# Sparse-attention indexer of a hybrid decoder step: the new tokens' index keys turned ahead of the last row block, their index products in one run, the head sums in four column groups

## The chip, the cores and the metric

The kernel runs on one core of a Trainium2 chip. The metric is the device time of one execution in microseconds (us), taken as the median of several executions. A core has five engines with a queue each: TensorE (matrix products; PE in the profile, its weight loads PEld), VectorE (DVE), ScalarE (ACT), GpSimd (POOL) and SyncE (SP, which only issues DMAs). An engine works through its queue in the order that the program was built with. Products are written to PSUM, a small memory that VectorE and ScalarE read.

## The reference, cut to what matters

One step of a decoder layer for 1024 prompt tokens and for 8 sequences with 4 new tokens each. The layer has sparse attention and retention side by side, merged by gates. The sparse attention first scores every key with a small "indexer" and then keeps the 256 best keys of each query:

```python
def index_scores(qi, wi, ki):
    s = jnp.einsum('bqhd,bsd->bqhs', qi, ki)               # 4 index heads of 64
    w = wi * (N_HEADS_IDX ** -0.5 * HEAD_DIM_IDX ** -0.5)
    return jnp.einsum('bqhs,bqh->bqs', jax.nn.relu(s), w)  # relu, then a weighted sum over the heads

def dsa_sample(...):                                        # the 8 sequences of new tokens
    ki_past = cache_kidx[page_table].reshape(DB, PAST_LEN, HEAD_DIM_IDX)
    ki_all = jnp.concatenate([ki_past, ki_new], axis=1)     # 1024 cached keys and 4 new ones
    idx, valid = select_keys(index_scores(qi, wi, ki_all), pos, topk)
    ...                                                     # attention over the chosen keys
```

All of it is in fp32. The index keys of the past lie in a paged cache, so that each sequence's 8 pages of 128 rows of 64 numbers must be gathered by a table.

## The kernel before, in words

**Order.** The program is traced in Python, and a planner lays out each engine's queue: from its own model of costs it takes, at each moment, the instruction that is ready and was traced first. `tc.issue_after(x)` keeps what it encloses behind instruction x on x's engine; it is an order in the queue and not a wait for x to end. The helper `together` (line 184) puts a list of products behind the first of them, so that once the first is placed the others are the next in line. Semaphores are set by the dependences of tiles: a tile of a pool with `bufs=n` takes the place of the n-th tile of its name before it, and waits until that one has been read.

**Projections.** Most of TensorE's time goes into projections of all 1056 tokens: 128 columns of weights at a time, the weights and the activations each split into a high and a low part (fp32r), three products per tile of 128 rows (lines 225 to 227), 24 products for each of three chunks of 352 tokens, 72 in all. ScalarE and VectorE or GpSimd split the weights one projection ahead (lines 210 and 211). The results lie in two PSUM banks `pj` in turn. The four "gate" projections (`gates`, lines 873 to 877, results copied by ScalarE in line 876) are traced behind the index stage, but are independent of it: the planner uses their products to fill TensorE while the index stage waits for other engines.

**Index stage, prompt.** The loop in lines 944 to 964 goes over row blocks b = 7 to 2 of 128 queries with widths of (b+1) x 128 keys, and over four heads: products into a two-bank PSUM tile `pl` (two such tiles, lines 952 and 953), relu by ScalarE into `rl` (two buffers, line 955), a weighted sum by VectorE into `SC[b]` (lines 957 and 959). Meanwhile GpSimd copies pages of the key cache (`copy_page`, line 582), one for each head after the first.

**Index stage, new tokens** (lines 967 to 1030). `gidx` holds the rows to be gathered. A small product with selectors builds `wsel`, which holds each query's head weights (lines 988 to 994). The 8 sequences are dealt with in two groups G of four:

- For each sequence b, GpSimd issues an indirect DMA of 256 KB into `kx` (line 1000, two buffers). TensorE turns it by four transposes into a PSUM bank `pt` (line 1006, two such banks), and ScalarE or VectorE copies the bank to `kp` (line 1008, five buffers).
- For each group, eight products of 64 rows, 32 query columns and 512 keys (line 1013) go to one `pl` tile: the halves o = 0 and 64 are the upper and lower 64 rows of the array and the two banks of the tile, b4 = 0 to 3 are four column groups of 32. Four more products handle the new keys in `kiT`, 32 columns wide (line 1016). Then ScalarE takes the relu into an `rl` tile (two strided pieces, line 1019, and a small one, line 1021).
- At the end, products with `wsel` sum over the heads of both groups: keys 0 to 511 in column group 0, keys 512 to 1023 in column group 1, the second group added to the first in PSUM (line 1026), and the 32 new keys (line 1027). ScalarE copies the two halves to `SCS` (line 1029), VectorE adds the mask to the new keys' part (line 1030).

Behind this stage its PSUM pool is closed and its banks are used by the retention stage (line 1142), and its SBUF is used by the search and by retention. The search for the 256th best score (`pick_all`, lines 1112 to 1136) reads `SC` and `SCS`; ScalarE and VectorE work through it in small steps during retention.

The lines that the change touches are 961 (where a mark is taken after each row block) and 995 to 1030.

Of the kernel before, what the change touches and what calls it, by code (L numbers as in the profile page):

```python
# [123 lines left out]
def _hybrid_step(ctx, tc, A, outs, dbg):  # L124
# [25 lines left out]
    def pl():  # L150
        return ps.tile([128, 1024], F32, name="pl", bufs=2)

    def pt():
        return ps.tile([128, 512], F32, name="pt", bufs=2)
# [89 lines left out]
    def last_on(engine):  # L244
        return next(i for i in reversed(nc.cur_bb.bb.instructions) if i.engine == engine)
# [638 lines left out]
    with ExitStack() as s1:  # L884
# [4 lines left out]
        with ExitStack() as s2:  # L889
# [52 lines left out]
            pages_of.append(pts)  # L942
            pages.extend((b, 2 * u + i) for G in (0, 1) for u in range(4) for b in range(4 * G, 4 * G + 4) for i in (0, 1))
            for b in range(7, 1, -1):
                W = (b + 1) * 128
                for h in range(4):
# [13 lines left out]
                    if h:  # L960
                        copy_page()
                if b == 7:
                    whole_row = scored.ins
# [31 lines left out]
            RL = []  # L995
            for G in (0, 1):
                KP = []
                for b in range(4 * G, 4 * G + 4):
                    kx = ip.tile([128, 8, 64], F32, name="kx", bufs=2)
                    nc.gpsimd.indirect_dma_start(  # L1000
                        out=kx.rearrange("p s d -> p (s d)"), out_offset=None,
                        in_=A["cache_kidx"][0].rearrange("g (r s) d -> (g r) (s d)", s=8),
                        in_offset=bass.IndirectOffsetOnAxis(ap=gidx[:, b:b + 1], axis=0))
                    p = pt()
                    for s in range(4):
                        nc.tensor.transpose(p[:, 128 * s:128 * s + 128], kx[:, 2 * s:2 * s + 2].rearrange("p a d -> p (a d)"), ident)
                    kp = ip.tile([128, 512], F32, name="kp", bufs=5)
                    (nc.vector.tensor_copy if b % 2 else nc.scalar.copy)(kp, p)
                    KP.append(kp)
                x, xn = pl(), pt()  # L1010
                for o in (0, 64):
                    for b4 in range(4):
                        nc.tensor.matmul(x[32 * b4:32 * b4 + 32, 8 * o:8 * o + 512], QF[o:o + 64, 4 * G + b4], KP[b4][o:o + 64],
                                         start=True, stop=True)
                for b4 in range(4):
                    nc.tensor.matmul(xn[32 * b4:32 * b4 + 32, :NS], QF[0:64, 4 * G + b4], kiT[0:64, T:], start=True, stop=True)
                rl = ip.tile([128, LK], F32, name="rl", bufs=2)
                for o in (0, 1):
                    nc.scalar.activation(rl[:, :PAST].rearrange("p (q s o) -> p o s q", s=4, o=2)[:, o],
                                         x[:, 512 * o:512 * o + 512].rearrange("p (s q) -> p s q", s=4), AF.Relu)  # L1020
                nc.scalar.activation(rl[:, PAST:], xn[:, :NS], AF.Relu)
                RL.append(rl)
            x, xn = pl(), pt()
            for G in (0, 1):
                for o, n0 in ((0, 0), (32, 512)):
                    nc.tensor.matmul(x[o:o + NS, n0:n0 + 512], wsel[:, G], RL[G][:, n0:n0 + 512], start=(G == 0), stop=(G == 1))
                nc.tensor.matmul(xn[:NS, :NS], wsel[:, G], RL[G][:, PAST:], start=(G == 0), stop=(G == 1))
            for o, n0 in ((0, 0), (32, 512)):
                nc.scalar.copy(SCS[:, n0:n0 + 512], x[o:o + NS, n0:n0 + 512])
# [714 lines left out]
```

## Time and profile before

| | |
|---|---|
| median of 3 runs | 1059.58 us (1057.87 to 1059.66) |
| profiled execution | 1059.82 us; 1058.2 us from its first to its last instruction |
| granted TensorE clock, mean | 0.995 |
| TensorE busy | 1034.1 us (98%) |
| weight loads of TensorE busy | 955.3 us (90%) |
| VectorE busy | 681.5 us (64%) |
| ScalarE busy | 451.7 us (43%) |
| GpSimd busy | 223.7 us (21%) |
| index stage, prompt row blocks | about 70 to 124 us from the start |
| index products of new tokens | 103.2 to 143.0 us |

A row of the order of time reads: start in us, length in us, engine, line of the kernel, operation, tile written <- tiles read, shapes, xcount of records that follow each other; in brackets the idle time before it and what ended that. A row of a group reads: line, engine, operation, tiles, shapes, xcount | time covered in us, mean length in ns | idle time before them. An fp32 product appears as two records; a transpose and an fp32r product as one. Records of TensorE overlap, since the next product starts before the last has drained; starts of neighbours say more than lengths. Only idle time of the engine that sets the end costs anything.

### The profile page before, as it was taken

The page shows a single profiled execution, that of the slowest core. Times are in us where ns is not written, and L with a number is a line of the kernel's source. Part 1 is how long each engine was busy: PE and PEld are TensorE (multiplying, and loading weights), DVE is VectorE, ACT ScalarE, POOL GpSimd, SP SyncE. Part 2 cuts the span into 40 slices and gives each one's busy share as a digit, 9 for nine tenths or more (in the row PEclk, how much of TensorE's full clock was granted, in tenths as well). Part 3 has the DMA queues.
Part 4 walks back from the last instruction along what each step waited for, and adds up shares of the span by engine and source line. Part 5 has one row for each costly group of instructions (what it writes and reads, how often), then busy time and mean ns, then how long its engine had stood idle before and what let it go on. Part 6 is the DMA issues. An engine that isn't in the chain of part 4 may idle for free. (4 is left out here: it accounts for less than half of the span.)

```text
span 1058.2 us, 20003 instructions
## 1 busy us (share of the span) xinstructions
PE 1034.1 (98%) x7758; PEld 955.3 (90%) x7758; DVE 681.5 (64%) x1533; ACT 451.7 (43%) x927; POOL 223.7 (21%) x192
## 2 busy tenths in 40 slices
PE   7999999999999999998999999999999999999996
PEld 6899889999999999997999998788999999998776
DVE  6876349788978787989435434111267676587665
ACT  5685445555644465232233322221356666433111
POOL 0016525113410311021200002433033333100000
PEclk9999999999999999999899999999999999999999
DMA  9936766365635634663598789678876421656531
GB/s 306 275 81 184 197 192 175 95 217 156 171 117 181 165 116 159 176 167 89 191 328 277 266 268 330 224 243 284 282 257 232 175 88 32 211 172 227 184 105 60
DMA packets 183907, 202.53 MB, mean 191 GB/s; under 512 B 24308, under 2 KB 153348, under 8 KB 182724
## 3 DMA queue, kind: packets, MB, share of 16 engines
q1 hardware_dynamic: 171520, 175.07, 52.4%
q0 software_dynamic: 11776, 25.32, 7.6%
q8 instruction: 61, 1.00, 0.4%
q10 hardware_dynamic: 516, 0.86, 0.2%
q14 instruction: 34, 0.28, 0.1%
HBM read 156.11 MB, written 57.95 MB: 202 GB/s over the span
## 5 line engine op out<-in xcount | busy, mean ns | idle before, releaser
L225 PE MATMUL pj<-hh,wh 128*128 128x352 f32 (+1 forms) x1168 | 383.9, 329 | 4.0 <-DVE rot L865 3.6
L226 PE MATMUL pj<-hl,wh 128*128 128x352 f32 (+1 forms) x1168 | 378.3, 324 | 0.0
L227 PE MATMUL pj<-hh,wl 128*128 128x352 f32 (+1 forms) x1168 | 377.9, 324 | 0.2 <-POOL wl L211 0.2
L225 PEld LDWEIGHTS pj<-hh,wh 128*128 128x128 f32 x1168 | 220.2, 188 | 14.2 <-issue 7.8
L226 PEld LDWEIGHTS pj<-hl,wh 128*128 128x128 f32 x1168 | 220.6, 189 | 5.4 <-issue 4.9
L227 PEld LDWEIGHTS pj<-hh,wl 128*128 128x128 f32 x1168 | 220.2, 189 | 4.4 <-issue 3.7
L1045 DVE TENSOR_SCALAR_CACHE_REDUCE eq<-sc,cand 128x896 bf16<-128x896 f32 (+4 forms) x155 | 135.8, 876 | 2.8
L210 ACT CAST wh<-ws 128x1024 fp32r<-128x1024 f32 (+1 forms) x65 | 61.1, 942 | 134.9 <-PE pj L226 89.4
L211 POOL TENSOR_TENSOR wl<-ws,wh 128x1024 fp32r<-128x1024 f32 x18 | 43.2, 2400 | 228.6 <-ACT wh L210 228.5
L211 DVE TENSOR_TENSOR wl<-ws,wh 128x1024 fp32r<-128x1024 f32 (+1 forms) x47 | 52.7, 1121 | 46.4 <-ACT wh L210 46.3
L1429 POOL TENSOR_SCALAR lg<-lg,st 128x1024 f32<-128x1024 f32 (+7 forms) x64 | 47.5, 763 | 109.9 <-DVE st L1426 100.3
L1264 DVE STREAM_TRANSPOSE kt<-kv 128x1024 f32<-128x1024 f32 x32 | 38.8, 1233 | 47.3 <-DMA kv<-KG 46.9
L1421 ACT ACTIVATE lg<-lg,st 128x1024 f32<-128x1024 f32 (+7 forms) x64 | 49.5, 774 | 28.8 <-DVE st L1415 24.5
L1655 PE MATMUL pj<-woh,MH 128*128 128x512 f32 (+1 forms) x136 | 51.4, 378 | 0.0
L1656 PE MATMUL pj<-wol,MH 128*128 128x512 f32 (+1 forms) x136 | 51.2, 377 | 0.0
L1657 PE MATMUL pj<-woh,ML 128*128 128x512 f32 (+1 forms) x136 | 51.2, 377 | 0.0
L1234 POOL DMA_INDIRECT kv<-in_cache_v,idx x32 | 31.8, 993 | 58.1 <-PE sx L1298 40.7
L1672 ACT ACTIVATE u<-xo 128x512 f32<-128x512 f32 (+2 forms) x19 | 11.6, 609 | 66.3 <-DVE xo L1671 44.0
L876 ACT ACTIVATE raw<-pj 128x352 f32<-128x352 f32 x48 | 22.1, 461 | 40.3 <-PE pj L227 36.0
L1052 ACT ACTIVATE ra<-sc,cand 128x1024 bf16<-128x1024 f32 x31 | 35.6, 1149 | 6.2 <-DVE cand L1128 4.3
L1052 ACT ACTIVATE ra<-scs,cand 32x1056 bf16<-32x1056 f32 x31 | 36.4, 1175 | 0.8
L1415 DVE CUSTOM_DVE_ANT_0 lg<-x,bi 128x512 f32<-128x512 f32 (+3 forms) x64 | 35.3, 570 | 1.5 <-PE x L1414 1.1
(385 smaller groups left out, 1840.5 us busy)
## 6 DMA issues: line engine op xcount, KB each, us to landing
ws<-in_w_in SPq DMA_DIRECT2D x49, 512.0 KB
kv<-KG SPq DMA_DIRECT2D x32, 512.0 KB
KG<-in_cache_k SPq DMA_DIRECT2D x40, 256.0 KB
rot<-in_rot SPq DMA_DIRECT2D x8, 1056.0 KB
x<-in_w_ada SPq DMA_DIRECT2D x16, 512.0 KB
TG<-raw SPq DMA_DIRECT2D x15, 528.0 KB
KG<-in_cache_k POOLq DMA_DIRECT2D x24, 256.0 KB, 6.6
wst<-in_w_out SPq DMA_DIRECT2D x12, 512.0 KB
```

The costliest lines, as they stand in the source:

```text
L210: nc.scalar.copy(wh[:, :, :n], ws[:, :, :n])
L211: (nc.vector if k == 4 or len(order) % 3 else nc.gpsimd).tensor_sub(wl[:, :, :n], ws[:, :, :n], f32(wh[:, :, :n]))
L225: nc.tensor.matmul(p, wh[:, k], HH[k][:, sl], start=(k == 0), stop=False)
L226: nc.tensor.matmul(p, wh[:, k], HL[k][:, sl], start=False, stop=False)
L227: nc.tensor.matmul(p, wl[:, k], HH[k][:, sl], start=False, stop=(k == KT - 1))
L1045: nc.vector.tensor_scalar(junk[:n, :W], sc, thr[:n, j:j + 1], 0.0, op0=op, op1=OP.add, accum_out=cnt[:n, j:j + 1])
L1052: nc.scalar.activation(junk[:n, :W], sc, AF.Sign, bias=thr[:n, NV + j:NV + j + 1], scale=-1.0, accum_out=cnt[:n, NV + j:NV + j + 1])
L1421: nc.scalar.activation(l, l, AF.Exp, bias=st[:, i, 1:2], scale=-1.0, accum_out=st[:, i, 3:4])
L1429: nc.gpsimd.tensor_scalar(l, l, st[:, i, 2:3], 0.5, op0=OP.mult, op1=OP.mult)
L1655: nc.tensor.matmul(x, MH[:, k, tk], wh[:, k], start=(k == 0), stop=False)
L1656: nc.tensor.matmul(x, MH[:, k, tk], wl[:, k], start=False, stop=False)
L1657: nc.tensor.matmul(x, ML[:, k, tk], wh[:, k], start=False, stop=(k == KT - 1))
```

## The change

It keeps what is computed, and changes four things in the index stage of the new tokens.

1. The gathers of all eight sequences are traced ahead of the transposes, with six buffers `kx` instead of two.
2. The four transposes of a sequence go out together, behind the last product of a given row block: sequences 0 and 1 behind block 5 (width 768), 2 and 3 behind block 4, 4 to 7 behind block 3 (width 512). There are eight buffers `kp` instead of five.
3. The index products of both groups, sixteen over cached keys and eight over new keys, are one list that goes out together behind the last product of row block 2, group 1 first. Then come the relus of both groups, the small one first. Both `pl` tiles and both `pt` banks are taken at once.
4. The head sums use four column groups of 256 keys each in one `pt` bank instead of two groups of 512 keys in a `pl` tile; group 1 is first and group 0 is added, and the two products for the new keys follow in the same list. VectorE copies the four quarters to `SCS`.

```diff
             pages_of.append(pts)
+            ends = {}
...
+                ends[b] = last_on(mybir.EngineType.PE)
                 if b == 7:
                     whole_row = scored.ins
...
-            RL = []
-            for G in (0, 1):
-                KP = []
-                for b in range(4 * G, 4 * G + 4):
-                    kx = ip.tile([128, 8, 64], F32, name="kx", bufs=2)
-                    nc.gpsimd.indirect_dma_start(
...
-                    p = pt()
-                    for s in range(4):
-                        nc.tensor.transpose(p[:, 128 * s:128 * s + 128], kx[:, 2 * s:2 * s + 2].rearrange("p a d -> p (a d)"), ident)
-                    kp = ip.tile([128, 512], F32, name="kp", bufs=5)
-                    (nc.vector.tensor_copy if b % 2 else nc.scalar.copy)(kp, p)
-                    KP.append(kp)
-                x, xn = pl(), pt()
-                for o in (0, 64):
-                    for b4 in range(4):
-                        nc.tensor.matmul(x[32 * b4:32 * b4 + 32, 8 * o:8 * o + 512], QF[o:o + 64, 4 * G + b4], KP[b4][o:o + 64],
-                                         start=True, stop=True)
-                for b4 in range(4):
-                    nc.tensor.matmul(xn[32 * b4:32 * b4 + 32, :NS], QF[0:64, 4 * G + b4], kiT[0:64, T:], start=True, stop=True)
+            KX = []
+            for b in range(NB):
+                kx = ip.tile([128, 8, 64], F32, name="kx", bufs=6)
+                nc.gpsimd.indirect_dma_start(
...
+                KX.append(kx)
+            KP = []
+            for b in range(NB):
+                p = pt()
+                with tc.issue_after(ends[(5, 4, 3, 3)[b // 2]]):
+                    together([lambda s=s: nc.tensor.transpose(p[:, 128 * s:128 * s + 128], KX[b][:, 2 * s:2 * s + 2].rearrange("p a d -> p (a d)"), ident)
+                              for s in range(4)])
+                kp = ip.tile([128, 512], F32, name="kp", bufs=8)
+                (nc.vector.tensor_copy if b % 2 else nc.scalar.copy)(kp, p)
+                KP.append(kp)
+            RL, xs_ = [], [(pl(), pt()) for _ in (0, 1)]
+            with tc.issue_after(ends[2]):
+                together([lambda o=o, b4=b4, G=G: nc.tensor.matmul(xs_[G][0][32 * b4:32 * b4 + 32, 8 * o:8 * o + 512], QF[o:o + 64, 4 * G + b4], KP[4 * G + b4][o:o + 64],
+                                                                   start=True, stop=True) for G in (1, 0) for o in (64, 0) for b4 in range(4)] +
+                         [lambda b4=b4, G=G: nc.tensor.matmul(xs_[G][1][32 * b4:32 * b4 + 32, :NS], QF[0:64, 4 * G + b4], kiT[0:64, T:], start=True, stop=True)
+                          for G in (0, 1) for b4 in range(4)])
+            for x, xn in xs_:
                 rl = ip.tile([128, LK], F32, name="rl", bufs=2)
+                nc.scalar.activation(rl[:, PAST:], xn[:, :NS], AF.Relu)
                 for o in (0, 1):
                     nc.scalar.activation(rl[:, :PAST].rearrange("p (q s o) -> p o s q", s=4, o=2)[:, o],
                                          x[:, 512 * o:512 * o + 512].rearrange("p (s q) -> p s q", s=4), AF.Relu)
-                nc.scalar.activation(rl[:, PAST:], xn[:, :NS], AF.Relu)
                 RL.append(rl)
-            x, xn = pl(), pt()
-            for G in (0, 1):
-                for o, n0 in ((0, 0), (32, 512)):
-                    nc.tensor.matmul(x[o:o + NS, n0:n0 + 512], wsel[:, G], RL[G][:, n0:n0 + 512], start=(G == 0), stop=(G == 1))
-                nc.tensor.matmul(xn[:NS, :NS], wsel[:, G], RL[G][:, PAST:], start=(G == 0), stop=(G == 1))
-            for o, n0 in ((0, 0), (32, 512)):
-                nc.scalar.copy(SCS[:, n0:n0 + 512], x[o:o + NS, n0:n0 + 512])
+            x, xn = pt(), pt()
+            together([lambda o=o, G=G: nc.tensor.matmul(x[32 * o:32 * o + NS, :256], wsel[:, G], RL[G][:, 256 * o:256 * o + 256], start=(G == 1), stop=(G == 0))
+                      for G in (1, 0) for o in range(4)] +
+                     [lambda G=G: nc.tensor.matmul(xn[:NS, :NS], wsel[:, G], RL[G][:, PAST:], start=(G == 0), stop=(G == 1)) for G in (0, 1)])
+            for o in range(4):
+                nc.vector.tensor_copy(SCS[:, 256 * o:256 * o + 256], x[32 * o:32 * o + NS, :256])
             nc.vector.tensor_tensor(SCS[:, PAST:], xn[:NS, :NS], C[:NS, C_MN:C_MN + 32], op=OP.add)
```

More of the change, by code (lines that the diff above doesn't have):

```diff
@@ L994, in _hybrid_step @@
                 nc.vector.tensor_reduce(wsel[:, G], t.rearrange("p h t -> p t h"), op=OP.add, axis=AX.X)
-            RL = []
-            for G in (0, 1):
-                KP = []
-                for b in range(4 * G, 4 * G + 4):
-                    kx = ip.tile([128, 8, 64], F32, name="kx", bufs=2)
-                    nc.gpsimd.indirect_dma_start(
-                        out=kx.rearrange("p s d -> p (s d)"), out_offset=None,
-                        in_=A["cache_kidx"][0].rearrange("g (r s) d -> (g r) (s d)", s=8),
-                        in_offset=bass.IndirectOffsetOnAxis(ap=gidx[:, b:b + 1], axis=0))
-                    p = pt()
-                    for s in range(4):
-                        nc.tensor.transpose(p[:, 128 * s:128 * s + 128], kx[:, 2 * s:2 * s + 2].rearrange("p a d -> p (a d)"), ident)
-                    kp = ip.tile([128, 512], F32, name="kp", bufs=5)
-                    (nc.vector.tensor_copy if b % 2 else nc.scalar.copy)(kp, p)
-                    KP.append(kp)
-                x, xn = pl(), pt()
-                for o in (0, 64):
-                    for b4 in range(4):
-                        nc.tensor.matmul(x[32 * b4:32 * b4 + 32, 8 * o:8 * o + 512], QF[o:o + 64, 4 * G + b4], KP[b4][o:o + 64],
-                                         start=True, stop=True)
-                for b4 in range(4):
-                    nc.tensor.matmul(xn[32 * b4:32 * b4 + 32, :NS], QF[0:64, 4 * G + b4], kiT[0:64, T:], start=True, stop=True)
@@ new lines, in _hybrid_step @@
+            KX = []
+            for b in range(NB):
+                kx = ip.tile([128, 8, 64], F32, name="kx", bufs=6)
+                nc.gpsimd.indirect_dma_start(
+                    out=kx.rearrange("p s d -> p (s d)"), out_offset=None,
+                    in_=A["cache_kidx"][0].rearrange("g (r s) d -> (g r) (s d)", s=8),
+                    in_offset=bass.IndirectOffsetOnAxis(ap=gidx[:, b:b + 1], axis=0))
+                KX.append(kx)
[8 more added lines that the diff above has]
+                KP.append(kp)
```

## The prediction

> **What bounds the kernel now.** I read the page first, then the busy time of each engine by stretches around the index stage, then the groups and the order of time of TensorE there. The page says that TensorE is the bound:
>
> ```profile
> span 1058.2 us, 20003 instructions
> PE 1034.1 (98%) x7758; PEld 955.3 (90%) x7758; DVE 681.5 (64%) x1533; ACT 451.7 (43%) x927; POOL 223.7 (21%) x192
> ```
>
> TensorE is idle for only 24 us of 1058.2. A gain must therefore come out of TensorE's own time, or out of one of its few waits. The stretches (columns: length, then busy time of PE, weight loads, DVE, ACT and POOL with the number of records, granted clock, DMA share, GB/s) show where this time is badly used:
>
> ```profile
> 84.00:124.50 40.50, 39.62 (x253) 37.98 (x252) 21.11 (x30) 20.09 (x44) 24.49 (x21) 1.00 0.66 189
> 124.50:143.25 18.75, 18.75 (x120) 11.55 (x119) 4.71 (x15) 7.74 (x18) 8.19 (x8) 1.00 0.85 235
> 143.25:150.00 6.75, 6.75 (x44) 6.75 (x44) 4.41 (x13) 4.28 (x9) 3.55 (x2) 1.00 0.65 207
> ```
>
> In the last row, where only projection products run, weight loads are busy all the time. From 124.5 to 143.25 us, where the new tokens' index products run, TensorE is "busy" all the time too, but it makes 120 records in 18.75 us (6.4 a us) against 44 in 6.75 (6.5) although most of the 62 others are narrow tiles that could share the array. The clock is full, so this is no throttling.
>
> How long do the index products hold TensorE there? The projection products (lines 225 to 227) are a measure, since they come at a fixed pitch:
>
> ```profile
> L227 PE MATMUL pj<-hh,wl 128*128 128x352 f32 x20 | 6.6, 331 | 0.0
> L226 PE MATMUL pj<-hl,wh 128*128 128x352 f32 x19 | 6.5, 343 | 0.0
> L225 PE MATMUL pj<-hh,wh 128*128 128x352 f32 x19 | 6.2, 329 | 0.0
> ```
>
> ```profile
> 124.56 0.33 PE L225 MATMUL pj<-hh,wh 128*128 128x352 f32 x1
> ...
> 143.22 0.32 PE L225 MATMUL pj<-hh,wh 128*128 128x352 f32 x1
> ...
> 146.10 0.32 PE L225 MATMUL pj<-hh,wh 128*128 128x352 f32 x1
> ...
> 146.58 0.32 PE L225 MATMUL pj<-hh,wh 128*128 128x352 f32 x1
> ```
>
> The groups are those of the stretch from 124.57 to 143.21. Three products take 146.58 - 146.10 = 0.48 us, so 0.16 each. From 124.56 to 143.22 there are 58 of them, 9.3 us; the rest of the 18.66 us, **9.4 us**, is what the index products of the new tokens hold, switching included.
>
> Why so long? An fp32 product shows as two records. Compare one product alone with eight together:
>
> ```profile
> 124.82 1.09 PE L1013 MATMUL pl<-kp,QF 64*32 64x512 f32 x16
> 125.84 0.43 PE L226 MATMUL pj<-hl,wh 128*128 128x352 f32 x1
> ...
> 130.95 1.04 PE L1013 MATMUL pl<-kp,QF 64*32 64x512 f32 x2
> 131.92 1.05 PE L1026 MATMUL pl<-rl,wsel 128*32 128x512 f32 x4
> ```
>
> Eight products on eight tiles (two row halves, four column groups) take 125.84 - 124.82 = 1.02 us; one alone takes 0.97. Group 0 went out in one run, but group 1 in pieces, each nearly at the price of a whole run, because its keys were turned one batch at a time between them.
>
> **The change part by part.**
>
> *One run of 16 + 8 products (A).* On each of the eight tiles two products now follow one another. The nearest row is line 1298: 16 records are 8 products on four column groups, again two per tile, 512 columns wide.
>
> ```profile
> 682.91 0.32 PE L227 MATMUL pj<-hh,wl 128*128 128x352 f32 x1
> 683.17 1.92 PE L1298 MATMUL sx<-kv,PS 128*32 128x512 f32 x16
> ...
> 685.29 0.32 PE L226 MATMUL pj<-hl,wh 128*128 128x352 f32 x1
> ...
> 621.63 1.93 PE L1243 MATMUL sx<-kt,QB 128*32 128x256 f32 x32
> 623.49 0.43 PE L226 MATMUL pj<-hl,wh 128*128 128x352 f32 x1
> ```
>
> From 682.91 to 685.29 there are two pitches, 0.32, and 2.06 us for the run with its switches. The eight 32-column products go in the same run:
>
> ```profile
> 102.91 0.32 PE L225 MATMUL pj<-hh,wh 128*128 128x352 f32 x1
> 103.16 0.27 PE L1016 MATMUL pt<-kiT,QF 64*32 64x32 f32 x8
> 103.36 0.41 PE L952 MATMUL pl<-kih,qs 128*128 128x320 f32 x1
> ```
>
> Four of them alone held TensorE for 103.36 - 102.91 - 0.16 = 0.29 us, most of it switching; eight inside a run I put at 0.3. So A is 2.4 us. Bounds: 2.1, if the small ones vanish beside the others; 4.4, if the two row halves do not share the array and A is four turns instead of two. I take 2.4, since the row at 124.82 shows the halves sharing.
>
> *Head sums in four column groups (B).* Two products of 256 columns per group in place of two of 512 on two groups. Line 1243 puts 16 products of 256 columns on four groups, four per group, in 623.49 - 621.63 = 1.86 us; two per group are 0.93, with 0.2 of switching 1.1, and two 32-column products 0.2: 1.3 us. Bounds 1.1 to 1.6.
>
> *Turning of the keys.* Eight groups of four transposes before and after; two of the old ones lie in the 9.4 us.
>
> ```profile
> 106.95 0.63 PE L1006 MATMUL pt<-C,kx 128*128 128x128 f32 x4
> 107.33 0.41 PE L225 MATMUL pj<-hh,wh 128*128 128x352 f32 x1
> 107.58 0.33 PE L226 MATMUL pj<-hl,wh 128*128 128x352 f32 x1
> ```
>
> A group costs 107.58 - 106.95 - 0.16 = 0.5 us. Two move ahead of 124 us: 1.0. The other six stay six (some of the old ones were torn, so a gain of 0.2 at most, which I leave out).
>
> *The wait for the gathered keys.* Two buffers before, six now, and the first turning stands behind the row block of width 768, which ends at 96.69:
>
> ```profile
> 96.69 0.34 PE L953 MATMUL pl<-kil,qs 128*128 128x384 f32 x1
> ...
> 97.67 0.32 PE L227 MATMUL pj<-hh,wl 128*128 128x352 f32 x1
> 98.87 0.65 PE L1006 MATMUL pt<-C,kx 128*128 128x128 f32 x4 [0.88 <-DMA kx<-in_cache_kidx,gidx]
> ...
> 115.57 0.39 PE L953 MATMUL pl<-kil,qs 128*128 128x512 f32 x1
> ...
> 123.91 0.34 PE L953 MATMUL pl<-kil,qs 128*128 128x384 f32 x1
> ```
>
> ```profile
> DMA to landing us min/median/max: 5.7/5.7/5.7
> ```
>
> The wait cost 98.87 - 97.67 - 0.16 = 1.0 us. Six gathers can now go out as soon as the indices are there, well before 96.69, so the wait goes. The seventh and eighth wait for a buffer until the first turnings, about 97 to 98 us, and land 5.7 us later, near 105; they are turned behind the block of width 512, which ends at 115.57. All eight copies can be done by 123.91, when the last row block leaves TensorE. GpSimd's queue holds page copies and some weight splits behind these gathers; a microsecond of delay there meets splits made a whole projection (72 products, 11.5 us) ahead. The new buffers (four and three of 2 KB a partition) cost nothing that I can see.
>
> *SCS copied by VectorE in four pieces instead of two by ScalarE.*
>
> ```profile
> 131.06 0.69 DVE L1008 COPY kp<-pt 128x512 f32<-128x512 f32 x1 [4.40 <-PE pt L1006]
> ```
>
> A copy of 512 columns takes 0.69 us, so four of 256 take at most 2.8. VectorE is busy for 4.71 of the 18.75 us there: it covers them, and no product waits for SCS but through the banks that the next stage takes over. Zero; up to 2.8 us if that cover goes.
>
> *The new wait.* B needs all of ScalarE's relus of both groups, which now stand together behind A:
>
> ```profile
> 122.85 0.46 ACT L876 ACTIVATE raw<-pj 128x352 f32<-128x352 f32 x1
> ...
> 137.40 2.15 ACT L1019 ACTIVATE rl<-pl 128x512 f32<-128x512 f32 x2 [2.77 <-PE pl L1013]
> ```
>
> Two take 2.15 us, four 4.3; with two small ones and what else stands in ScalarE's queue I take 5. TensorE must have projection products to fill that. The row at 122.85 copies out the last third of the third gate (the ninth of twelve such copies), so the fourth gate, 72 products or 11.5 us of work, starts about when A does. Whether the order written out by the planner puts enough of them (some 30) between A and B is the open point: 0 if yes, 5 if none. I take 0.3, because in the profile above the same chain from line 1013 over 1019 to 1026 has no wait on TensorE. What queues behind B on TensorE is all that follows; ScalarE and VectorE have slack.
>
> **The sum.** Removed: 9.4 (stretch) + 0.3 (first four small products) + 1.0 (wait) = 10.7. Added: 2.4 + 1.3 + 1.0 + 0.3 = 5.0. Net 5.7 us, against the profiled execution's own 1059.82 (its span and 1.6 around it): 1054.1. That execution was 0.24 above the median shown, 1059.58, so 1054.0 for the median.
>
> The Trainium skill (Perfetto Trace Analysis, Identifying the Most-Contended Engine) says to judge TensorE by how long its weight loads are busy and not by its matmul time. By that rule the stretch has 18.75 - 11.55 = 7.2 us of room instead of the 4.7 that I take from it, and the time could come to about 1051.5.
>
> **The rivals.**
>
> *B waits.* If few products lie between A and B, up to 5 us come back: 1055 to 1059. For it: a planner that counts the sixteen products one after the other would see the first group's relus done before A ends, and leave few fillers. Against it: today's chain shows no such wait. A long wait has a second price in this trace:
>
> ```profile
> PE pj L225 <- DVE rot L865: 3.6, 1, 3.6
> ```
>
> ```profile
> 499.00:503.00 4.00, 0.43 (x3) 0.19 (x2) 4.00 (x5) 1.40 (x2) 0.00 (x0) 0.81 0.50 121
> 503.00:507.00 4.00, 4.00 (x14) 4.00 (x15) 3.93 (x11) 0.00 (x0) 0.00 (x0) 0.50 0.94 317
> ```
>
> After a wait of 3.6 us the granted clock was 0.50 for the next 4 us, so 2 us more were lost; a whole wait of 5 would end at 1054.0 + 4.7 + 2 = 1060.7, no change. The Trainium skill (TensorE: Matmul & The Clock Gate, Part 1) has this as a rule: after about 3.4 us of idleness the clock is halved, in windows that run free of the kernel; the trace agrees with its 0.50. By that rule a wait below about 3 us costs only itself.
>
> *Absorbed later.* The stage from 540 to 660 us loads much:
>
> ```profile
> 540.00:660.00 120.00, 118.32 (x943) 108.34 (x943) 56.21 (x71) 35.45 (x85) 14.69 (x10) 1.00 0.88 296
> ```
>
> With DMA at 0.88, TensorE could arrive 5.7 us early and wait there for keys: 1059.7. Against it: TensorE is busy for 118.32 of 120 us, and the loads are issued behind others that wait for TensorE's own progress, so they move with it.
>
> *The run is torn (the other side).* The sixteen products leave piecemeal, as the key tiles come one by one, as group 1 does now. Each further piece costs about 1.1 us (0.97 and a switch). Six pieces eat the gain, and from eight on the kernel is slower by over 2.1 us; all sixteen alone would be 16 x 1.1 = 17.6 instead of 2.1, giving 1069. It happens if the last gathers land only after 123.91. For it: the profile shows group 1 torn in just this way. Against it: the landing near 105 worked out above, and a first product that needs the bank of the last row-block head.
>
> **How the numbers follow.** 0.2% is 2.1 us, about what can be told from no change, so "same" is 1057.5 to 1061.7. The forecast, 1051 to 1056: 0.56. B waits: 0.17, of it 0.12 below 1057.5 and 0.05 above. Absorbed: 0.07. Torn: 0.15. Better than 1051, by the room that the weight loads show or a shifted wait at 500 us that spares the halved clock: 0.05. Faster 0.56 + 0.12 + 0.05 = 0.73; same 0.05 + 0.07 = 0.12; slower 0.15. The range from 1051.0 to 1061.5 leaves out the 0.05 below and the torn run above; the likeliest case alone has 1051 to 1056.
>
> **What would show it.** Right: one block of 48 records of the lines that hold the index products, from 2.1 to 2.7 us long; one of 20 for the head sums near 1.3; no wait of TensorE on the gathered keys; the stage's end some 6 us earlier, and everything behind it earlier by as much. Wrong: a wait of TensorE on ScalarE's relus ahead of the head sums (first rival); longer waits on the transposed keys after 540 us (second); several small blocks of index products or late gathers (third); or waits elsewhere in the span that the new order of the instructions brings in.

## The result and the profile after

The changed kernel takes 1052.76 us (median; 1050.89 to 1056.29), the kernel before, timed beside it, 1059.62 us (1057.87 to 1061.55). The ratio is 0.9938, with an interval of 0.9922 to 0.9953: 5.0 to 8.3 us faster. The forecast was 1054.0, with 1051.0 to 1061.5 as its range.

The six executions of the changed kernel lie 5.4 us apart, about as much as the change is worth. The profiled execution of the changed kernel is its longest, 1056.29 us. So I don't compare whole executions first, but one stretch that holds all that was changed: from the first product of the prompt's row blocks (line 952 before, 953 after) to the first product of retention's scores (line 768). In order of time on TensorE, of before:

```profile
67.18 0.39 PE L952 MATMUL pl<-kih,qs 128*128 128x512 f32 x1
...
190.96 0.45 PE L768 MATMUL pb<-qrT,krT 64*64 64x128 f32 x8
```

and of after:

```profile
67.14 0.39 PE L953 MATMUL pl<-kih,qs 128*128 128x512 f32 x1
...
185.21 0.45 PE L768 MATMUL pb<-qrT,krT 64*64 64x128 f32 x8
```

Before, the stretch takes 190.96 - 67.18 = 123.78 us, after 185.21 - 67.14 = 118.07: **5.71 us less**. The working of the prediction had 5.7. In a second profiled execution of the changed kernel the stretch comes within 0.2 us of this (the table further below), and between the two instructions TensorE has the same 576 projection products to do before and after; so this is the number that the experiments can be read by.

The page of after, and its stretches (columns as in the prediction: length, then PE, weight loads, VectorE, ScalarE and GpSimd with their records, granted clock, DMA share, GB/s):

```profile
PE 1031.8 (98%) x7766; PEld 958.9 (91%) x7766; DVE 685.3 (65%) x1537; ACT 450.0 (43%) x925; POOL 222.9 (21%) x192
```

```profile
84.00:124.50 40.50, 40.50 (x257) 39.26 (x255) 25.39 (x34) 20.94 (x47) 25.22 (x21) 1.00 0.70 196
124.50:134.00 9.50, 8.69 (x101) 6.96 (x101) 0.58 (x3) 5.29 (x12) 5.58 (x5) 1.00 0.93 280
134.00:150.00 16.00, 16.00 (x102) 16.00 (x101) 12.11 (x35) 5.76 (x11) 5.58 (x4) 1.00 0.77 217
```

TensorE's busy time fell by 2.3 us (1034.1 to 1031.8), the span of this execution by 3.6; the rest is idle time. The index stage is now over at about 134 us instead of 143. From 134 us on weight loads are busy for all of 16.00 us, which is how pure projection work looks. The row block stretch (84 to 124.5) has lost its idle time: 40.50 busy of 40.50, against 39.62. New is the idle time in the middle row, 9.50 - 8.69 = 0.8 us.

In order of time on TensorE, after:

```profile
97.05 0.34 PE L954 MATMUL pl<-kil,qs 128*128 128x384 f32 x1
97.22 1.03 PE L1009 MATMUL pt<-C,kx 128*128 128x128 f32 x8
...
98.24 0.31 PE L954 MATMUL pl<-kil,qs 128*128 128x320 f32 x1
...
124.30 0.32 PE L225 MATMUL pj<-hh,wh 128*128 128x352 f32 x1
124.55 1.49 PE L1016 MATMUL pl<-kp,QF 64*32 64x512 f32 x20
...
126.38 0.43 PE L1018 MATMUL pt<-kiT,QF 64*32 64x32 f32 x10
...
127.01 0.32 PE L227 MATMUL pj<-hh,wl 128*128 128x352 f32 x1
...
131.31 0.32 PE L227 MATMUL pj<-hh,wl 128*128 128x352 f32 x1
132.44 1.07 PE L1028 MATMUL pt<-rl,wsel 128*32 128x256 f32 x16 [0.81 <-ACT rl L1024]
...
133.81 0.32 PE L226 MATMUL pj<-hl,wh 128*128 128x352 f32 x1
```

The keys of two sequences (line 1009, eight transposes) are turned right behind a row block and wait for nothing. The sixteen index products (line 1016) and the eight small ones (line 1018) stand in one run: from 124.30 to 127.01 are two pitches of 0.16 and **2.39 us** for the run. Then 29 projection products follow, and the head sums (line 1028) wait 0.81 us, by the bracket for ScalarE's relu of line 1024.

### The profile page after: what moved, and what is told of

It reads as the page before. It is cut to its first block, busy times and chain, and to the rows that moved or that the text cites. A ratio compares the mean times of both kernels' runs of the same rounds, so it can differ in the third digit from the quotient of the medians.

```text
span 1054.6 us, 20021 instructions
## 1 busy us (share of the span) xinstructions
PE 1031.8 (98%) x7766; PEld 958.9 (91%) x7766; DVE 685.3 (65%) x1537; ACT 450.0 (43%) x925; POOL 222.9 (21%) x192
```

## The experiments

Each kernel's stretch from the first row-block product to line 768, beside its whole time (medians):

| kernel | first row block, us | line 768, us | stretch | less than before | median time | ratio to before, interval |
|---|---|---|---|---|---|---|
| before | 67.18 | 190.96 | 123.78 | | 1059.62, 1060.08, 1060.29 | |
| after | 67.14 | 185.21 | 118.07 | 5.71 | 1052.76 | 0.9922 to 0.9953 |
| after again | 66.37 | 184.29 | 117.92 | 5.86 | 1052.77 | 0.9914 to 0.9953 |
| head sums alone | 67.12 | 189.46 | 122.34 | 1.44 | 1058.83 | 0.9976 to 0.9999 |
| early keys alone | 68.34 | 188.29 | 119.95 | 3.83 | 1056.84 | 0.9961 to 0.9984 |
| after, old sums | 69.52 | 188.10 | 118.58 | 5.20 | 1052.69 | 0.9909 to 0.9943 |
| after, six page tiles | 65.98 | 183.41 | 117.43 | 6.35 | 1052.40 | 0.9899 to 0.9944 |
| after, two key buffers | 66.43 | 187.53 | 121.10 | 2.68 | 1056.71 | 0.9953 to 0.9982 |
| after, banks exchanged | 65.56 | 183.43 | 117.87 | 5.91 | 1051.35 | 0.9895 to 0.9940 |
| both of these edits | 65.72 | 183.15 | 117.43 | 6.35 | 1050.00 | 0.9888 to 0.9936 |

The starts of the row blocks already differ by 4 us (65.56 to 69.52), though none of these edits touches the work ahead of them. The stretch behind them repeats within 0.2 us where the edits do not reach into it (after, its repeat and the exchanged banks: 117.87 to 118.07). There is one profiled execution of each of the others.

### The changed kernel again

No edit. It serves to tell what repeats from what does not.

> The changed kernel once more, nothing edited. Theory (the gain is made in the index stage, and what differs between executions is the granted clock after the few waits of TensorE): at 155 us from the start it is again 5.7 to 5.8 us ahead of the kernel before, since nothing random lies there; executions differ by up to 5 us, and the slow ones are those with the lower mean clock (0.992 to 0.994, 1053 to 1056 us) and the quick ones those with the higher (0.996 to 0.998, 1050 to 1052 us). Rival (the change itself causes the loss of 2.8 us that the first profile shows between 370 and 406 us): the same two waits of 0.8 and 1.5 us stand at 370 and 382 us again, and the lead falls from 5.75 to about 2.9 us there again.

Measured: 1052.77 us, ratio 0.9934 (0.9914 to 0.9953). The stretch is 5.86 us shorter. TensorE's wait ahead of the head sums is there again, with 0.65 us. So are, later, waits of 0.50 us at 368.47 (line 678), 1.48 us at 380.41 (line 768) and 2.94 us at 497.14 (line 225). What did not come again is a fall of the granted clock at 380 to 388 us. The rows of after, and below those of its repeat:

```profile
380.00:384.00 4.00, 2.51 (x23) 2.20 (x23) 3.42 (x7) 2.26 (x2) 0.05 (x1) 0.88 0.48 139
384.00:388.00 4.00, 4.00 (x28) 3.88 (x29) 1.84 (x5) 2.27 (x4) 0.00 (x0) 0.69 0.34 102
```

```profile
380.00:384.00 4.00, 3.59 (x34) 3.42 (x35) 2.42 (x5) 2.44 (x4) 0.00 (x0) 1.00 0.34 100
384.00:388.00 4.00, 4.00 (x48) 3.71 (x47) 3.96 (x10) 3.35 (x6) 0.00 (x0) 1.00 0.30 98
```

In the first execution, 4 us at 0.88 and 4 at 0.69 lost 0.5 + 1.2 = 1.7 us; in the repeat the clock stayed at 1.00 behind the same wait. In these two executions the waits came with the kernel, and the fall of the clock with one execution. The rival, that the lead falls to about 2.9 us there each time, is not borne out: at the next product of line 797 (395.04 us before, 392.12 in after, 389.33 in the repeat) the lead, counted from the same first product of the row blocks, is 2.88 us in after and 4.90 in the repeat. The waits alone cost the repeat about 1 us of its lead. As expected, the longest executions of this run have the lowest mean clock (1056.72 us at 0.991, 1054.45 at 0.993) and the shortest the highest (1050.96 and 1051.74 at 0.997).

### Head sums alone

```diff
-            x, xn = pl(), pt()
-            for G in (0, 1):
-                for o, n0 in ((0, 0), (32, 512)):
-                    nc.tensor.matmul(x[o:o + NS, n0:n0 + 512], ...
...
+            x, xn = pt(), pt()
+            together([lambda o=o, G=G: nc.tensor.matmul(x[32 * o:32 * o + NS, :256], ...
...
+            for o in range(4):
+                nc.vector.tensor_copy(SCS[:, 256 * o:256 * o + 256], x[32 * o:32 * o + NS, :256])
```

The kernel before, with part 4 of the change and nothing else.

> The kernel before with the head sums alone changed (four column groups of 256 keys, one list, four copies by VectorE); keys, gathers and index products as before. Theory: the head sums hold TensorE for 1.2 us in place of about 2.6, so the lead at 155 us is 1.2 to 1.5 us, 1058.3 for the median; the index products stay torn. Rival (the sums were hidden behind other work or their gain goes into a wait for the relus): lead at 155 us under 0.5 us, a wait of TensorE ahead of the sums.

Measured: the stretch is 1.44 us shorter; 1058.83 us, ratio 0.9988 (0.9976 to 0.9999). The index products stay as they were. In order of time on TensorE:

```profile
127.84 1.04 PE L1013 MATMUL pl<-kp,QF 64*32 64x512 f32 x2
...
142.29 1.07 PE L1024 MATMUL pt<-rl,wsel 128*32 128x256 f32 x16
```

Group 1 still comes in pieces (two records are one product), and the sums (here line 1024) go out last, with no idle time ahead of them; from 142.03 to 143.66, less two pitches, they hold TensorE for 1.3 us. So where the sums need not wait, this part is worth what was expected of it, 1.2 to 1.5 us, and the rival (under 0.5 us, a wait ahead of the sums) falls.

### Early keys alone

```diff
+            for b in range(NB):
+                kx = ip.tile([128, 8, 64], F32, name="kx", bufs=6)
...
+                with tc.issue_after(ends[(5, 4, 3, 3)[b // 2]]):
+                    together([lambda s=s: nc.tensor.transpose(p[:, 128 * s:128 * s + 128], ...
...
             for G in (0, 1):
-                KP = []
...
```

The kernel before with parts 1 and 2: gathers and turnings early and in their places. The index products, relus and sums are still traced group by group, without a list and without a pin.

> Gathers with six buffers, turned in fours behind the row blocks as in the change, but index products, relus and head sums written as before, group by group and without a list. Theory (group 1 was torn only because its keys came late): the products of both groups stand together all the same, about 2.4 to 2.9 us for all of them in place of about 6.2; with the wait for the keys (1.0) and whole groups of transposes (0.5) that frees 4.8 to 5.3 us, but the head sums of group 0 follow only 10 products (1.6 us) later, so that TensorE should wait 1 to 3 us for the relus: lead at 155 us 2 to 4 us. Rival (the list and the pin behind the last row block make the single run): the products stay torn, lead at 155 us 1.5 to 2 us, made of the wait and the transposes only.

Measured: the stretch is 3.83 us shorter; 1056.84 us, ratio 0.9972 (0.9961 to 0.9984). In order of time on TensorE (products in line 1019, sums in 1032):

```profile
125.75 1.09 PE L1019 MATMUL pl<-kp,QF 64*32 64x512 f32 x16
...
126.69 1.21 PE L1019 MATMUL pl<-kp,QF 64*32 64x512 f32 x15
...
131.27 1.05 PE L1032 MATMUL pl<-rl,wsel 128*32 128x512 f32 x4 [1.70 <-ACT rl L1027]
```

The products of both groups stand in one block here too, though nothing tells the planner to put them there: with the keys in place, all of them are ready at once. Once the keys are there early, the list and its pin are therefore not what makes the run. The old sums wait 1.70 us for the relus: only nine projection products stand between the index products and the first of them.

### The change without its head sums

```diff
-            x, xn = pt(), pt()
-            together([lambda o=o, G=G: nc.tensor.matmul(x[32 * o:32 * o + NS, :256], ...
+            x, xn = pl(), pt()
+            for G in (0, 1):
+                for o, n0 in ((0, 0), (32, 512)):
...
```

> The changed kernel with the head sums as before (two column groups of 512 keys, a pl tile, copies by ScalarE). Theory: the block of 48 records stays at 2.4 us and the sums cost 2.6 instead of 1.2 us; the wait of 1.0 us for the relus may shrink since the two groups are summed one after the other: lead at 155 us 4.4 to 5.3 us. Rival (the lead needs the sums in one list, since broken sums cost a switch each): lead under 4 us.

Measured: the stretch is 5.20 us shorter, 0.5 to 0.7 less than with the new sums, and the time is 1052.69 us, ratio 0.9926 (0.9909 to 0.9943), the same as the whole change within what can be told. In order of time on TensorE, the sums (here line 1030):

```profile
133.50 1.05 PE L1030 MATMUL pl<-rl,wsel 128*32 128x512 f32 x4
...
135.06 1.05 PE L1030 MATMUL pl<-rl,wsel 128*32 128x512 f32 x4
```

Alone the new sums are worth 1.44 us, on top of the rest only a third to half of it. The difference is the wait ahead of them: here TensorE does not wait at the sums, which go out in pieces as each group's relus are done; the four-column sums need all the relus at once. From 132.72 to 136.31 us, less five projection products between them, the old sums hold TensorE for 2.8 us; the new ones hold it for 1.3 and make it wait 0.9 (both worked out below).

Beside the early keys alone, this kernel has the list with its pin and the small relus first, and it is 1.37 us quicker (5.20 against 3.83): the sums no longer stand so close behind the products. So the list is worth something, though not by making the run; its parts were not run singly.

### Page-number tiles

Why do the relus come so late? ScalarE's queue in after, in order of time, from the first copy of page numbers that waits to the first relu:

```profile
124.93 0.19 ACT L596 COPY ptn<-pts 8x1 int32<-8x1 int32 x1 [1.07 <-POOLq L600]
126.78 0.19 ACT L596 COPY ptn<-pts 8x1 int32<-8x1 int32 x1 [1.66 <-POOLq L600]
128.18 0.19 ACT L596 COPY ptn<-pts 8x1 int32<-8x1 int32 x1 [1.21 <-POOLq L600]
128.28 1.15 ACT L1024 ACTIVATE rl<-pl 128x512 f32<-128x512 f32 x1
```

TensorE goes on to projection products at 126.74, but the first relu starts at 128.28. Ahead of it in the queue stand copies of eight numbers (`ptn<-pts`, 0.2 us each). There are two tiles for them, and each copy waits until GpSimd has read the tile of two copies before (POOLq, line 600), and GpSimd takes one for each page that it copies, here 1.85 and 1.40 us apart. The edit changes only the number of tiles; the order of instructions on every engine stays the same.

```diff
-            t = cst.tile([NB, 1], I32, name="ptn", bufs=2)
+            t = cst.tile([NB, 1], I32, name="ptn", bufs=6)
```

> The changed kernel with six buffers instead of two for the little tiles of page numbers (ptn, line 594); the order of the instructions on every engine is the same. Theory (the relus start late because ScalarE's queue, strictly in order, holds three tiny copies of page numbers ahead of them, each waiting for GpSimd to have read the tile before): the copies no longer wait, the first relu starts with the first products, about 126.5 us instead of 128.28, and TensorE's wait ahead of the head sums (0.8 us in the profile of after, 0.65 in its repeat) is gone; the lead over before at 150 us is 6.3 to 6.6 us instead of 5.7 to 5.9; median 0.6 us below the changed kernel, which the spread hides. Rival (four relus of 1.07 us and two small ones are too long for what stands between the products and the sums, whatever stands ahead of them): the wait stays at 0.6 us or more and the lead at 5.7.

Measured, in order of time on ScalarE and on TensorE:

```profile
122.57 0.55 ACT L596 COPY ptn<-pts 8x1 int32<-8x1 int32 x5
125.68 1.17 ACT L1024 ACTIVATE rl<-pl 128x512 f32<-128x512 f32 x1 [2.57 <-PE pl L1016]
```

```profile
130.34 0.32 PE L227 MATMUL pj<-hh,wl 128*128 128x352 f32 x1
130.59 1.07 PE L1028 MATMUL pt<-rl,wsel 128*32 128x256 f32 x16
...
131.96 0.32 PE L226 MATMUL pj<-hl,wh 128*128 128x352 f32 x1
```

The five copies go out in one go, the first relu starts 2.17 us after the run's first product (123.51 in this trace) instead of 3.73, and TensorE does not wait any more. The stretch is 6.35 us shorter, 0.5 to 0.65 better than the change alone. The rival (relus simply too long) falls: 29 projection products are enough for four relus. The median, 1052.40, cannot tell 0.6 us.

The same rows give the price of the sums without a wait: from 130.34 to 131.96 is 1.62, less two pitches of 0.16 is **1.30 us**.

### Two key buffers

```diff
-                kx = ip.tile([128, 8, 64], F32, name="kx", bufs=6)
+                kx = ip.tile([128, 8, 64], F32, name="kx", bufs=2)
```

> The changed kernel with two buffers for the gathered keys, as before, instead of six. Everything else, the list and its pin included, stands; the last two gathers can now go out only behind the turning of the fifth and sixth key tile. In the written order the sixteen products now stand in three pieces (2, then 1 with 3 small ones, then 13 with 5 small ones) with projection products between. Theory (keys that are there early make the run): the products cost 1.1 us more for each of the two further pieces, 4.0 to 5.0 us instead of 2.4, and the first turnings wait about 1 us again for their gather if two gathers are no earlier than before; lead at 150 us 2.2 to 4.0 us. Rival (the run is made by the list and its pin, and the wait was not the buffers'): cost 2.4 to 2.8, no wait, lead 5.3 or more.

Measured: the stretch is only 2.68 us shorter than before; 1056.71 us, ratio 0.9968 (0.9953 to 0.9982). In order of time on TensorE:

```profile
117.86 0.30 PE L1009 MATMUL pt<-C,kx 128*128 128x128 f32 x1 [2.77 <-DMA kx<-in_cache_kidx,gidx]
...
126.53 0.32 PE L225 MATMUL pj<-hh,wh 128*128 128x352 f32 x1
126.78 1.05 PE L1016 MATMUL pl<-kp,QF 64*32 64x512 f32 x4
...
128.03 0.32 PE L227 MATMUL pj<-hh,wl 128*128 128x352 f32 x1
...
128.51 0.32 PE L227 MATMUL pj<-hh,wl 128*128 128x352 f32 x1
...
131.09 0.32 PE L226 MATMUL pj<-hl,wh 128*128 128x352 f32 x1
```

The first turnings do not wait, contrary to what was expected. The wait is at the sixth key tile, and it is 2.77 us: with two buffers its gather can go out only when the fourth tile has been turned, about 107 us, and in GpSimd's queue it came at 109.94. Then the last two tiles are turned after 123.8 us, where the run should have started, and the run falls into two pieces (the second and third of the written order left as one). The first, two products, is as dear as a run of eight: from 126.53 to 128.03 are two pitches and 1.18 us. The second takes 131.09 - 128.51 - 0.32 = 2.26, together 3.44 us instead of 2.39, where 4.0 to 5.0 had been expected of three pieces. The wait and the tear, 2.77 + 1.05, less what the wait at the sums costs in after (0.9) and in its repeat (0.7), which is not there, are 2.9 to 3.1 of the 3.0 to 3.2 us that are lost against the change. Buffers that let the gathers start early are over half of what the change is worth. Without them the new order waits 2.77 us for a gather, where the old order waited 0.88; whether the pinned turnings or the new order of the gathers lengthens the wait was not separated.

### Banks exchanged at 490 us

What the changed kernel still waits for, by waits from 140 us on (in total, times, longest):

```profile
PE pj L225 <- DVE rot L865: 3.0, 1, 3.0
PE sx L1246 <- DVE kt L1267: 1.5, 1, 1.5
PE pb L768 <- DVE tmp L774: 1.5, 1, 1.5
```

The first of these is the next projection chunk, which asks for the bank `pj3` while VectorE has still to read the last of four updates of the retention state from it. The two products that VectorE reads first can use that bank instead:

```diff
-        po, pn = two(), [pt(), pt()] + apart()
+        po, pn = apart(), [pt(), pt()] + two()
```

> The changed kernel with the new tokens' two sums of the state (po) and their last two updates (pn) exchanged between PSUM banks, line 853: the bank that the next projection chunk asks for (pj3) is then freed by VectorE's first two multiplications instead of by the last of its four updates. Theory (what the changed kernel still loses, and most of its spread from run to run, lie in TensorE's wait at about 500 us and in the clock behind it): the wait of 2.99 us (2.94 to 3.57 in the other profiles) falls below 0.5, the granted clock stays above 0.9 from 498 to 506 us instead of 0.50 to 0.64, the lead over before grows by 4 to 5 us there, and the median is 1047.5 to 1049.5; the spread falls below 4 us. Rivals: the wait only moves to the next bank (1052 to 1053); the wait goes but the clock is low at that place whatever the wait (1049.5 to 1050.5).

Measured: 1051.35 us (1049.89 to 1053.27), ratio 0.9917 (0.9895 to 0.9940). The wait did not go; it moved on by nearly 7 us (it ends 12.3 us behind the turning of line 868 instead of 5.6) and is hardly shorter:

```profile
PE pj L225 <- ACT qs L619: 2.7, 1, 2.7
```

The 20 us around it, in after and then in this kernel:

```profile
486.00:506.00 20.00, 16.43 (x106) 13.96 (x105) 19.89 (x35) 3.21 (x7) 0.49 (x1) 0.83 0.35 106
```

```profile
486.00:506.00 20.00, 16.72 (x118) 15.02 (x111) 19.89 (x33) 3.87 (x9) 2.12 (x1) 1.00 0.50 147
```

In both rows VectorE (third engine) is busy for 19.89 of 20 us: it is the bound of this place, and TensorE is held up at the next bank whose readers stand behind VectorE's queue. The copy that TensorE waits for had itself waited for VectorE:

```profile
502.34 0.74 ACT L619 COPY qs<-pj 32x32 f32<-32x32 f32 x4 [8.24 <-DVE raw L616]
```

The rival "the wait only moves" is right about the wait; its time, 1052 to 1053, is a little high, the theory's 1047.5 to 1049.5 too low. The executions lie 3.4 us apart, within the 4 that the theory allowed. The granted clock over these 20 us is 1.00 here and 0.83 in after, which is up to 3.4 us of full speed; whether the edit earned that is a question for the last section.

### Both edits

```diff
-            t = cst.tile([NB, 1], I32, name="ptn", bufs=2)
+            t = cst.tile([NB, 1], I32, name="ptn", bufs=6)
...
-        po, pn = two(), [pt(), pt()] + apart()
+        po, pn = apart(), [pt(), pt()] + two()
```

> Both edits together: six buffers for the page-number tiles and the exchange of the banks. By both theories the gains add up, 0.6 and 4 to 5 us: median 1047 to 1049, lead at 150 us 6.3 to 6.6. By the rivals no more than the better of the two alone.

Measured: 1050.00 us (1048.72 to 1053.71), ratio 0.9912 (0.9888 to 0.9936), the lowest median of all. The stretch is 6.35 us shorter, as with the page tiles alone. The median is 1.0 us above the theories' range, since the wait stayed, and 1.35 below the better edit alone, which the spread could hide. The intervals of this kernel and of the change alone overlap (0.9888 to 0.9936 and 0.9914 to 0.9953), so that it beats the kernel before is shown, and that it beats the change is likely, not shown.

## Why the prediction was right, step by step

**The sum of the stretch** was 5.7 us and is 5.71, 5.86 in the repeat. The terms that count were right in kind: one run, cheaper sums, no wait for keys. That the total is met so closely is partly luck, since one term was 0.6 us too small and several small ones made up for it:

| step of the prediction | forecast | measured | from |
|---|---|---|---|
| old products and sums, taken away | 9.4 | 9.6 | 124.56 to 143.22 before, less 57 projection products |
| first four small products, taken away | 0.3 | 0.4 | 102.91 to 103.61 before, less 0.16 and 0.15 |
| one run of 16 + 8 products (A) | 2.4 | 2.39 | 124.30 to 127.01 in after |
| head sums in four column groups (B) | 1.3 | 1.30 | 130.34 to 131.96, six page tiles |
| two turnings moved | 1.0 | 0.86 | 97.05 to 98.24 in after, less one product of each width (0.18 and 0.15) |
| wait for gathered keys gone | 1.0 | gone | no idle time ahead of line 1009 |
| new wait of B | 0.3 | 0.88 | 131.31 to 133.81 less two pitches and 1.30 |
| six turnings that stay | 0 | 0.1 less | all 32 transposes: 3.8 before, 3.5 after |
| copies of SCS by VectorE | 0 | 0 | below |

*A* came out as its row said: eight tiles (two row halves, four column groups) work side by side, two turns of them cost two turns. The upper bound, four turns, is excluded.

*The new wait of B* is the term that was mis-sized: 0.9 us instead of 0.3. The prediction took it from the old chain, which had no wait, and counted ScalarE's load (four relus, 4.3 us, and "what else stands in ScalarE's queue") without asking what these other instructions wait for. They were three copies of 0.2 us that kept the queue waiting for 1.07 + 1.66 + 1.21 = 3.9 us. The rival *B waits* had the place right and the reason wrong: not few projection products (there were 29 between, some 30 were wanted), but a late start of the relus. Its long version, 5 us with a halved clock behind it, did not occur. The 0.6 us too little here was balanced by small terms. The largest is a miscount in the old stretch. The group's 58 projection products take in one that starts ahead of the stretch and only ends in it:

```profile
124.40 0.32 PE L227 MATMUL pj<-hh,wl 128*128 128x352 f32 x1
```

So 57 stand between 124.56 and 143.22, 9.1 of the 18.66 us, and the index products held 9.6 us and not 9.4. The first small products, with the switches on both sides, held 0.4 instead of 0.3. All 32 transposes (each group start to start, less the pitches of its neighbours) took 3.8 us before, without the wait, and 3.5 after; the prediction had set all of them at the same price before and after. With the measured terms the sum is 9.6 + 0.4 + 1.0 = 11.0, less 2.39 + 1.30 + 0.86 + 0.88 = 5.4, and 0.1 more for the six turnings that stayed: 5.7.

*The buffers* cost nothing visible and earn more than was put to them: the prediction had 1.0 us for the wait that they remove, and counted the run as a part of its own, though its rival of the torn run did hang it on the landing of the gathers. With two buffers TensorE waits 2.77 us for a gather and the run is torn; with six, the run forms even without a list. The gathers went out as worked out, six at once and two after the first turnings. The six stand from 81.27 us on; here are GpSimd's sixth and seventh gather:

```profile
88.18 0.95 POOL L1000 DMA_INDIRECT kx<-in_cache_kidx,gidx  x1 [0.30 <-issue]
99.07 1.11 POOL L1000 DMA_INDIRECT kx<-in_cache_kidx,gidx  x1 [0.31 <-PE pl L954]
```

The prediction had "about 97 to 98 us" for the last two; the seventh went out at 99.07.

*SCS by VectorE* was set to nothing with VectorE's idle time as cover:

```profile
133.57 1.71 DVE L1032 COPY scs<-pt 32x256 f32<-32x256 f32 x4 [8.90 <-PE pt L1028]
```

VectorE stood idle for 8.90 us before these four copies, which take 1.71 (2.8 had been the bound).

*By the weight loads.* By the rule of the Trainium skill (Perfetto Trace Analysis, Identifying the Most-Contended Engine) the stretch would have had 7.2 us to give, where the prediction took 4.7 from it. With the 1.0 of the wait for keys that is 8.2 in all, and the time could have come to about 1051.5. The changed kernel gave 5.7 and, without the page-number stalls, 6.35. In the row of 124.50 to 134.00 weight loads are busy for 6.96 of 8.69 us of TensorE's busy time: the run and the sums still keep 1.7 us in which no weights are loaded. The rule pointed the right way, and the reading of it as room promised 1.9 to 2.5 us more than came.

**The rivals.** *The run is torn* did not happen in the changed kernel, and happened when the buffers were taken away, at about the price it had been given: 1.18 us for a piece of two products, against 1.1. Two pieces are far from the six that would have eaten the gain. *Absorbed later* had 540 to 660 us as its place. Of the waits, the row of before that answers to after's line 1246 above:

```profile
PE sx L1243 <- DVE kt L1264: 1.3, 2, 0.9
```

1.3 us in two waits before, 1.5 in one after and 1.7 in its repeat: 0.2 to 0.4 us, not 5.7. What is given back is given back earlier, at 366 to 388 us. In after's profile, line 768's wait for VectorE (1.5 us against 1.2 before) and line 678's (0.8, none before) take 1.1 us together and the fallen clock another 1.7; in the repeat the same two waits took 0.8 us more than before's, and the clock nothing. In return the wait at 500 us, 3.57 before, is 2.99 in after and 2.94 in the repeat; that 0.6 us was in no sum, though the prediction names such a shift among its chances.

**The median** fell by 6.9 us against the runs taken beside it, where 5.7 were forecast. The interval of the ratio, 5.0 to 8.3 us, holds both; what the stretch does not account for is within what the starts (4 us apart) and the clock do to single executions. That a part of it is a true further gain later on is neither shown nor excluded.

## What to carry to other kernels

An instruction of 0.2 us can be the longest thing in a queue: before costing a new wait, read what stands ahead of the releasing instruction on its engine, and what each of those waits for in turn; here four more buffers of a tile of eight numbers took the wait away. Operands that are ready early let a planner form a dense run by itself, while a pinned order with late operands makes everything wait behind it (2.77 us here); so the buffers come first and the list second. Where whole executions differ by as much as the change is worth, measure from one fixed instruction to another around the change: the stretch repeated within 0.2 us where the medians needed an interval of 3 us.

## What the runs showed of the hardware that was not expected

Waits of the same length were followed by very different clocks. The Trainium skill (TensorE: Matmul & The Clock Gate, Part 1) states that the clock is halved after about 3.4 us of idleness, judged in a window that runs free of the kernel; the prediction drew from it that a wait below 3 us costs only itself. After waits of 2.99 us at 499.94 in after and of 2.99 us at 499.99 with two key buffers, the granted clock was:

```profile
498.00:502.00 4.00, 2.06 (x7) 2.06 (x8) 4.00 (x11) 0.00 (x0) 0.00 (x0) 0.64 0.59 146
502.00:506.00 4.00, 4.00 (x16) 4.00 (x15) 4.00 (x7) 0.19 (x2) 0.49 (x1) 0.51 0.66 261
```

```profile
498.00:502.00 4.00, 2.01 (x12) 2.02 (x13) 4.00 (x11) 0.00 (x0) 0.00 (x0) 1.00 0.58 141
502.00:506.00 4.00, 4.00 (x27) 4.00 (x26) 4.00 (x7) 0.16 (x1) 0.44 (x1) 1.00 0.69 268
```

The clock is the number behind the five engines: 0.64 and 0.51 in one, 1.00 and 1.00 in the other, with the same wait at the same time. So the length of the single wait does not decide here, and that a wait below 3 us costs only itself does not hold: waits of 2.94 us were followed by 0.50 in the repeat of the change and by 0.85 with six page tiles; 2.70 and 2.67 us in the two kernels with the banks exchanged by 1.00. At 380 us a wait of 1.49 us, 12 us after another of 0.78, was followed by 0.69 in after; the same place kept 1.00 in the repeat. None of these waits reaches the 3.4 us of the Trainium skill, and four were followed by less than the full clock; a window that runs free of the kernel would fit that the outcome changes from one execution to the next, but no run here shows the window itself. The price in after: the 20 products from 499.94 to 505.95 us take 6.0 us where 0.16 each would make 3.2, 2.8 us on top of the wait of 2.99. So the exchange of banks cannot be credited with its clock of 1.00. The spread of the executions goes with the clock: the six executions of the changed kernel took 1050.89, 1051.41 and 1051.76 us at a mean clock of 0.996 to 0.998, and 1053.76, 1055.11 and 1056.29 us at 0.992 to 0.994; a difference of 0.004 in the mean clock is 4 us of 1053.
